# Value columns accumulated beside the modulation, filters and gates beside query and gate columns, in a hybrid mixer block

## The chip, the cores and the metric

The kernel runs on one core of a Trainium2 chip. The core has a matrix engine (PE), a vector engine (DVE), a scalar engine (ACT), a general engine (POOL) and a queue engine (SP), each with its own instruction stream; they meet through semaphores. Loads go from the chip's memory into on-chip memory (SBUF) through DMA queues; PE writes its products into a small accumulator memory (PSUM) of eight banks. The metric is the device time of one execution in microseconds.

## The reference

One layer of a diffusion backbone, float32, with 256 tokens of context and 256 latent tokens of 2048 channels. Cut to what matters here:

```python
mod_l = split(silu(c) @ w_mod + b_mod, 6)         # w_mod [2048, 12288]
mod_c = split(silu(c_ctx) @ w_mod + b_mod, 6)
h_ctx, h_lat = ctx * (1 + mod_c[1]) + mod_c[0], x * (1 + mod_l[1]) + mod_l[0]
hy, q, k, v, o, gates, u, mg = split(h @ w_in)    # w_in [2048, 12304], k, v, u for both streams
y_ml = mlstm(q, k, v, gates, o)                   # q, k through a short convolution
y_s5 = s5(u)                                      # a complex diagonal state space, both directions
y_hy = hyena(hy)                                  # long convolutions with filters from a small network
merged = sum(sigmoid(g) * (y @ w) for g, y, w in branches)    # g: three thirds of mg
x = norm(ALPHA * x + mod_l[2] * (merged @ w_out))
x = norm(ALPHA * x + mod_l[5] * (relu(modulate(x, mod_l[3], mod_l[4]) @ w_ff1) ** 2 @ w_ff2))
```

The first two parts of the modulation are wanted before any product with w_in; the other four are wanted behind the mixer and in the feed-forward part.

## The kernel before

All weights are float32 and pass once through the core in chunks of 512 KB. A chunk is loaded on SP's queue into a tile `wr` (four buffers, L155), split into a high part `wh` by ACT and a low part `wl` by DVE (three buffers each, both at L145 and L149 in `split`), and multiplied by PE in three products for each pair of k and column tile: high by high, high by low, low by high. `lin_w` computes a block of columns of the projection into one PSUM tile `mm`, of which there are two with two banks each; `px` and `aux`, two banks each, serve everything else. A block for both streams is 256 columns wide and has four chunks of four k, a block for the latent stream alone is 512 columns wide and has eight chunks of two k. When a block's products are done a consume function reads the tile. `lin_w_steps` yields between chunks, and `run_steps(steps, n)` runs n chunks of it. Side work is written as generators in three slots; `chunk_done`, behind each chunk, advances each by its rate, so that `with_side(gen, 1.75, 1)` runs 1.75 parts of a generator per chunk. A scheduler then sets a fixed order for each engine from the order in the program and the buffers; an instruction waits for those ahead of it on its engine.

The stages, in the order of the program. `phase0(g)` for g from 0 to 3: `mod_block` streams 16 chunks of the first part of the modulation (four products with the stream's chunk in columns of the array, not split), then `h_group` makes four channel tiles of the modulated and transposed inputs. Beside group g of the modulation stand three key chunks, with the four k that group g - 1 has made; `part` adds the products of four k at a time in SBUF (copy by ACT the first time, then an add by DVE, L1504), since a PSUM tile would be needed for each block otherwise. Then come the last four k of the three key blocks and `k_consume`; the value columns V in 12 chunks with three kinds of side work: `gates`, `mod_late` (the rest of the modulation, by DVE alone at L1226, two products to a chunk, summed over k in the single buffer `mac`; 128 chunks in 16 blocks; PE adds up the rows of `mac` into `px` behind each block) and `hy_filters`; the query columns Q, 12 chunks; `mlstm`; the U columns, 12 chunks, whose consume copies on ACT and issues eight small DMAs for each column tile (L611); the O columns, 12; six hyena chunks; `s5_inject`; the other hyena chunks and 32 chunks of the merge gates (mg, 96 in all, `mg_consume` to DRAM) beside the scan on POOL; 48 more beside `s5_output`, whose first product is at L714; the rest of mg beside `hyena`; the three merges; the product with w_out, ahead of which `need_mods(12)` runs `mod_late` on until 96 of its chunks are done; and the feed-forward part, ff1 and ff2, between which `drain(1)` runs what is left of it.

## Time and profile before

| what | value |
|---|---|
| device time, median of 3 runs | 2071.19 us |
| lowest and highest | 2070.89, 2072.36 us |
| span of the profiled execution | 2066.5 us |
| PE busy | 1908.3 us, 92% |
| DVE busy | 1373.0 us, 66% |
| ACT busy | 799.8 us, 39% |
| POOL busy | 526.1 us, 25% |
| read from memory | 414.58 MB, 211 GB/s with what is written |

The span runs from the first to the last instruction of the profiled execution; the device time has what lies around it as well. Products on PE are pipelined, and a row's duration overlaps that of the next. The table by stage has, for each stretch, the busy time of each engine and in brackets the number of instructions, then PE's granted clock as a share of full speed, and the share of the DMA engines' time.

### The profile page before, as it was taken

What the parts mean: (1) busy time and instruction counts of PE and PEld (TensorE: products, weight loads), DVE (VectorE), ACT (ScalarE), POOL (GpSimd) and SP (SyncE); (2) the same over time, 40 slices, a digit from 0 to 9 for tenths busy, and PEclk for the clock granted to TensorE, in tenths of its full rate; (3) what the DMA queues carried; (4) which work ended last, traced back from release to release, by engine and by line L of the source; (5) the groups of instructions that cost most, each with busy time, mean ns of one, the idle gap of its engine ahead of it and who ended that gap; (6) DMA issues with size and microseconds to landing.
All of it is one profiled execution on the core that took longest, in us unless ns stands there. A gap on an engine that the chain in (4) does not pass through costs nothing.

```text
span 2066.5 us, 34948 instructions
## 1 busy us (share of the span) xinstructions
PE 1908.3 (92%) x14085; PEld 1733.0 (84%) x14085; DVE 1373.0 (66%) x1840; ACT 799.8 (39%) x1066; POOL 526.1 (25%) x656
## 2 busy tenths in 40 slices
PE   6889999999888999589988999799999999999995
PEld 2657988989888898579878978799989899998985
DVE  5567877547989855495688766966665555555556
ACT  1323333236444333234433443544443334444331
POOL 3435211000435799960243410500000000000001
PEclk7889999999999999789999999999999999999998
DMA  9777676766666676447766776577776666667663
GB/s 303 244 246 255 200 230 221 228 183 193 219 193 192 209 243 221 130 141 224 265 210 199 263 264 208 178 237 236 231 245 188 191 186 184 183 182 229 192 185 101
DMA packets 243378, 435.64 MB, mean 211 GB/s; under 512 B 22431, under 2 KB 69225, under 8 KB 242225
## 3 DMA queue, kind: packets, MB, share of 16 engines
q1 hardware_dynamic: 221744, 382.29, 59.1%
q0 software_dynamic: 11968, 43.26, 6.2%
q10 hardware_dynamic: 9504, 7.87, 1.4%
q8 instruction: 110, 1.80, 0.4%
q14 instruction: 52, 0.42, 0.1%
HBM read 414.58 MB, written 21.92 MB: 211 GB/s over the span
## 4 chain that ended last, share of the span: by engine, by line
PE 40%; DVE 9%; POOL 8%; DMA 6%; issue 2%; ACT 1%; POOLq 0%; ACTq 0%; DVEq 0%
PE mm L166 39%; DVE wl L149 3%; POOL sc L678 2%; POOL t L681 2%; DMA wr<-in_w_mod_dram 2%; POOL sc L680 2%; DMA wr<-in_w_out_dram 2%; POOL sc L679 2%; ACT wh L145 1%; DVE t L149 1%; DMA wr<-in_w_in_dram 1%; DVE mac L1226 1%; PE aux L166 1%; DMA wr<-in_w_hy_out_dram 1%; DVE b L707 0%
## 5 line engine op out<-in xcount | busy, mean ns | idle before, releaser
L166 PE MATMUL mm<-t,wh 128*128 128x256 f32 x5888 | 1112.5, 289 | 13.2 <-DVE t L149 7.0
L166 PEld LDWEIGHTS mm<-t,wh 128*128 128x128 f32 x5888 | 937.8, 195 | 39.5 <-issue 13.9
L149 DVE TENSOR_TENSOR wl<-wr,wh 128x1024 fp32r<-128x1024 f32 (+1 forms) x517 | 666.0, 1293 | 392.6 <-ACT wh L145 392.1
L145 ACT ACTIVATE wh<-wr 128x1024 fp32r<-128x1024 f32 (+1 forms) x517 | 546.3, 1058 | 841.2 <-PE mm L166 584.5
L166 PE MATMUL mm<-t,wl 128*128 128x256 f32 x2944 | 849.9, 289 | 19.0 <-DVE wl L149 18.8
L166 PEld LDWEIGHTS mm<-t,wl 128*128 128x128 f32 x2944 | 572.7, 195 | 31.5 <-DVE wl L149 23.2
L1226 DVE SCALAR_TENSOR_TENSOR mac<-wr,sc,mac 128x512 f32<-128x512 f32 x240 | 189.7, 790 | 143.6 <-DMA wr<-in_w_mod_dram 141.0
L166 PE MATMUL mm<-wh,t 128*128 128x512 f32 (+1 forms) x960 | 247.5, 347 | 0.0
L166 PEld LDWEIGHTS mm<-wh,t 128*128 128x128 f32 x960 | 168.2, 189 | 23.3 <-ACT wh L145 1.1
L166 PE MATMUL mm<-wl,t 128*128 128x512 f32 (+1 forms) x480 | 168.3, 351 | 5.3 <-DVE wl L149 5.2
L166 PE MATMUL mm<-wh,ff 128*128 128x512 f32 (+1 forms) x576 | 155.3, 358 | 0.0
L166 PEld LDWEIGHTS mm<-wh,ff 128*128 128x128 f32 x576 | 101.8, 188 | 17.6
L166 PEld LDWEIGHTS mm<-wl,t 128*128 128x128 f32 x480 | 90.8, 189 | 22.3 <-DVE wl L149 11.0
L166 PE MATMUL mm<-wl,ff 128*128 128x512 f32 (+1 forms) x288 | 103.0, 357 | 0.0
L1448 POOL DMA_DIRECT2D t<-in_ln_g_dram x1 | 0.5, 532 | 355.9 <-PE mm L166 355.9
L166 PE MATMUL mm<-ty,wh 128*128 128x256 f32 x384 | 73.3, 289 | 0.0
L166 PE MATMUL mm<-ty,wl 128*128 128x256 f32 x192 | 56.7, 296 | 8.5 <-DVE wl L149 8.3
L166 PEld LDWEIGHTS mm<-ty,wh 128*128 128x128 f32 x384 | 60.9, 192 | 0.9
L166 PEld LDWEIGHTS mm<-wl,ff 128*128 128x128 f32 x288 | 54.2, 188 | 8.8
L1237 POOL DMA_DIRECT2D mrow<-b x8 | 4.0, 500 | 224.0 <-DVE b L1235 224.0
L371 PE MATMUL px<-wr,b 128*32 128x512 f32 x128 | 40.6, 723 | 13.5 <-DMA wr<-in_w_mod_dram 13.5
L166 PE MATMUL aux<-t,t 128*128 128x384 f32 (+3 forms) x160 | 47.2, 411 | 5.4 <-DMA t<-HX 1.9
(458 smaller groups left out, 1937.2 us busy)
## 6 DMA issues: line engine op xcount, KB each, us to landing
wr<-in_w_ff_dram SPq DMA_DIRECT2D x256, 512.0 KB, 4.0
wr<-in_w_in_dram SPq DMA_DIRECT2D x192, 512.0 KB, 4.5
wr<-in_w_mod_dram SPq DMA_DIRECT2D x160, 512.0 KB, 4.8
wr<-in_w_out_dram SPq DMA_DIRECT2D x32, 512.0 KB, 4.6
wh<-in_w_mod_dram SPq DMA_DIRECT2D x16, 512.0 KB, 6.0
wl<-in_w_mod_dram SPq DMA_DIRECT2D x16, 512.0 KB, 6.9
MG<-mg POOLq DMA_DIRECT2D x24, 256.0 KB, 4.4
wr<-in_w_ml_out_dram SPq DMA_DIRECT2D x12, 512.0 KB, 4.5
```

Source lines behind the costliest of these rows:

```text
L145: return self.nc.scalar.activation(out, in_, f, bias=bias, scale=scale)
L149: self.nc.vector.tensor_sub(lo, x, hi.bitcast(F32))
L166: self.nc.tensor.matmul(out, lhsT, rhs, start=start, stop=stop, skip_group_check=True)
L371: nc.tensor.matmul(ps[o:o + 32], self.st[:, k, :], raw[:, kk, :], start=k < 4, stop=k >= KT - 4, skip_group_check=True, tile_position=(0, o))
L678: v.tensor_mul(t1, self.a8[:, 0], S[:, :, :, :, n - 1])
L679: v.tensor_mul(t2, self.a8[:, 1], S[:, :, ::-1, :, n - 1])
L680: v.tensor_add(t1, t1, S[:, :, :, :, n])
L681: v.tensor_add(S[:, :, :, :, n], t1, t2)
L1226: v.scalar_tensor_tensor(acc, x, c, acc, op0=ALU.mult, op1=ALU.add)
L1237: nc.gpsimd.dma_start(self.mrow[which // 3:which // 3 + 1, o:o + 512], brow)
L1448: nc.gpsimd.dma_start(g2r, I["ln2_g"].to_broadcast([P, D]))
```

## The change

`part` takes a list of accumulators in place of one. Beside the three key blocks there are three value blocks with accumulators of their own in SBUF: the fourth tile of `room`, and four half tiles under the tags "mg" (three) and "mac" (one). In `phase0` six steps stand among the 16 modulation chunks of a group, behind chunks 3, 6, 8, 11, 14 and 16, three key and three value chunks in turn; there were three, behind 3, 7 and 11. Behind `k_consume` the last four k of each value block and `v_consume` follow. The side work that stood beside V now stands beside Q and the first 12 chunks of mg, which are called right behind Q; `mod_late` has rate 0.6 there and `hy_filters` 1.2 as before. The later calls of 32, 48 and 96 mg chunks are as they were.

```diff
-                    if n % 4 == 3 and todo:
+                    if n in (3, 6, 8, 11, 14, 16) and todo:
                         step, k0 = todo.pop(0)
                         step(k0)
-            for step, k0 in todo:
-                step(k0)
...
-        def part(i, c0):
-            acc = self.room[i][:, :4, :]
+        def part(accs, c0):
+            n = 4 // len(accs)
...
                 once(k0, True)
-                if k0 == 0:
-                    self.act(acc, ps)
-                else:
-                    nc.vector.tensor_add(acc, acc, ps)
+                for i, acc in enumerate(accs):
+                    p = ps[:, n * i:n * i + n, :]
+                    if k0 == 0:
+                        self.act(acc, p)
+                    else:
+                        nc.vector.tensor_add(acc, acc, p)
...
-            kparts = [part(i, O_K + 256 * i) for i in range(3)]
-            self.ksteps = [step for _, step in kparts]
+            kparts = [part([self.room[i][:, :4, :]], O_K + 256 * i) for i in range(3)]
+            one = lambda tag, bufs: self.t(self.sm, [P, 512], tag, bufs).rearrange("p (s t) -> p s t", s=2)
+            vaccs = [[self.room[3][:, :4, :]], [one("mg", 3), one("mg", 3)], [one("mg", 3), one("mac", 1)]]
+            vparts = [part(a, O_V + 256 * i) for i, a in enumerate(vaccs)]
+            self.ksteps = [step for _, step in kparts + vparts]
...
                     gates = self.gates()
                     next(gates)
+                    for i, (accs, step) in enumerate(vparts):
+                        step(12)
+                        for j, acc in enumerate(accs):
+                            n = 2 // len(accs)
+                            self.v_consume(2 * i + n * j, n, acc)
                     self.with_side(gates, 0.5)
-                    self.with_side(self.mod_late(), 1.75, 1)
+                    self.with_side(self.mod_late(), 0.6, 1)
                     self.with_side(self.hy_filters(), 1.2, 2)
-                    self.lin_w_all(w_in, O_V, W, KT, both, self.v_consume)
+                    self.qT = self.t6([P, CT, T])
+                    self.lin_w_all(w_in, O_Q, W, KT, lat, self.q_consume)
                     self.drain()
-                    self.qT = self.t6([P, CT, T])
-                    self.sides[1][1] = 0.3
-                    self.lin_w_all(w_in, O_Q, W, KT, lat, self.q_consume)
+                    steps = self.lin_w_steps(w_in, O_MG, 3 * D, KT, lat, self.mg_consume)
+                    self.run_steps(steps, 12)
                     self.drain(2)
...
-                steps = self.lin_w_steps(w_in, O_MG, 3 * D, KT, lat, self.mg_consume)
```

How the order moves, first on PE where the U columns begin. Before, `mm_464` is the last block of Q, `aux` rows are the mLSTM's products, and `mm_531` is the first block of U:

```order
L166 MATMUL mm_464_3437<-t32_24_112,wl_479_3541 128x256
L166 MATMUL mm_464_3437<-t32_24_112,wh_478_3540 128x256 x2
L166 MATMUL mm_464_3437<-t32_24_112,wl_479_3541 128x256
L166 MATMUL aux_481_3577<-t6_406_3093,t6_252_1732 128x256 x2
L166 MATMUL aux_481_3577<-t6_406_3093,t6_253_1733 128x256
L166 MATMUL aux_482_3583<-t6_406_3093,t6_252_1732 128x256 x2
L166 MATMUL mm_531_3884<-t32_23_111,wh_533_3887 128x256 x2
L166 MATMUL mm_531_3884<-t32_23_111,wl_534_3888 128x256
L166 MATMUL mm_531_3884<-t32_24_112,wh_533_3887 128x256 x2
```

After, `mm_502` is the second block of mg, `px` the row sum of a late modulation block, the `aux` rows products of the filters and of the mLSTM; `mm_569` (not shown) is the first block of U:

```order
L166 MATMUL mm_502_3791<-t32_24_112,wh_515_3892 128x256
L166 MATMUL mm_502_3791<-t32_24_112,wl_516_3893 128x256
L166 MATMUL px_578_4349<-mac_464_3603,ones_8_79 1x512
L166 MATMUL aux_473_3626<-ty_347_2815 128x384
L166 MATMUL aux_474_3629<-ty_347_2815 128x384
L166 MATMUL aux_482_3669<-ty_344_2812,b4_343_2810 128x384
L166 MATMUL aux_481_3668<-ty_344_2812,b4_343_2810 128x384
L166 MATMUL aux_490_3711<-ty_344_2812,b4_343_2810 128x384
L166 MATMUL aux_489_3710<-ty_344_2812,b4_343_2810 128x384
```

And later on PE, in the scan, with the last rows of a hyena block `mm_1026`:

```order
L169 MATMUL aux_782_6160<-consts_14_90,s5q_778_6128 128x128 x2
L169 MATMUL aux_782_6160<-consts_14_90,s5q_779_6135 128x128 x2
L166 MATMUL mm_1026_7492<-t32_24_112,wl_1051_7626 128x256
L166 MATMUL mm_1026_7492<-t32_24_112,wh_1050_7625 128x256 x2
L166 MATMUL mm_1026_7492<-t32_24_112,wl_1051_7626 128x256
L166 MATMUL mm_502_3791<-t32_24_112,wh_1061_7683 128x256 x2
L166 MATMUL mm_502_3791<-t32_24_112,wl_1062_7684 128x256
```

The block `mm_502` stops after four of its eight chunks ahead of U, and goes on behind `mm_1026`.

On ACT where the first block of U is read out, before (`mm_531`):

```order
L145 ACTIVATE wh_548_4070<-wr_547_4068 128x1024
L145 ACTIVATE wh_555_4151<-wr_554_4149 128x1024
L145 ACTIVATE wh_562_4219<-wr_561_4217 128x1024
L145 ACTIVATE wh_567_4278<-wr_566_4276 128x1024
L145 ACTIVATE b2_551_4126<-mm_531_3884 128x8x64
L611 DMA UD_1_72<-b2_551_4126 16x8x64 x8
L145 ACTIVATE b2_552_4137<-mm_531_3884 128x8x64
L145 ACTIVATE wh_572_4340<-wr_571_4338 128x1024
L611 DMA UD_1_72<-b2_552_4137 16x8x64 x8
```

and after (`mm_569`):

```order
L145 ACTIVATE wh_587_4420<-wr_586_4418 128x1024
L145 ACTIVATE wh_595_4505<-wr_594_4503 128x1024
L145 ACTIVATE wh_599_4563<-wr_598_4561 128x1024
L145 ACTIVATE wh_604_4625<-wr_603_4623 128x1024
L145 ACTIVATE b2_591_4480<-mm_569_4232 128x8x64
L611 DMA UD_1_72<-b2_591_4480 16x8x64 x8
L145 ACTIVATE b2_592_4491<-mm_569_4232 128x8x64
L611 DMA UD_1_72<-b2_592_4491 16x8x64 x8
L145 ACTIVATE wh_610_4689<-wr_609_4687 128x1024
```

The copies `b2<-mm` stand behind the same number of weight splits in both; there is one split fewer between the second copy and its DMA issues.

On DVE where ff1 ends and ff2 begins, before (`wl_2106` is ff2's first split, `px_2100` the row sum of the last block of the modulation):

```order
L1226 SCALAR_TENSOR_TENSOR mac_2049_15120<-wr_2095_15533,sc_17_97,mac_2049_15120 128x512
L149 TENSOR_TENSOR wl_2091_15476<-wr_2089_15473,wh_2090_15475 128x1024
L1226 SCALAR_TENSOR_TENSOR mac_2049_15120<-wr_2095_15533,sc_17_97,mac_2049_15120 128x512
L1226 SCALAR_TENSOR_TENSOR mac_2049_15120<-wr_2097_15542,sc_17_97,mac_2049_15120 128x512
L149 TENSOR_TENSOR wl_2094_15506<-wr_2092_15503,wh_2093_15505 128x1024
L1226 SCALAR_TENSOR_TENSOR mac_2049_15120<-wr_2097_15542,sc_17_97,mac_2049_15120 128x512
L1226 SCALAR_TENSOR_TENSOR mac_2049_15120<-wr_2098_15546,sc_17_97,mac_2049_15120 128x512 x2
L1226 SCALAR_TENSOR_TENSOR mac_2049_15120<-wr_2099_15550,sc_17_97,mac_2049_15120 128x512 x2
L149 TENSOR_TENSOR wl_2106_15566<-wr_2104_15563,wh_2105_15565 128x1024
L149 TENSOR_TENSOR wl_2109_15584<-wr_2107_15581,wh_2108_15583 128x1024
L1235 TENSOR_TENSOR b2_2101_15556<-b2_2101_15556,px_2100_15554 1x512
```

and after, from behind the bias add of block 14 (it reads `px_2102`) and the first product of block 15, `mac_2104` (L1224); `wl_2119` is ff2's first split:

```order
L1400 TENSOR_TENSOR b4_2099_15535<-b4_2099_15535 128x1024
L1226 SCALAR_TENSOR_TENSOR mac_2104_15554<-wr_2105_15555,sc_17_97,mac_2104_15554 128x512
L1226 SCALAR_TENSOR_TENSOR mac_2104_15554<-wr_2106_15559,sc_17_97,mac_2104_15554 128x512
L149 TENSOR_TENSOR ff_1982_14508<-b4_2099_15535,ff_1982_14508 128x1024
L1226 SCALAR_TENSOR_TENSOR mac_2104_15554<-wr_2106_15559,sc_17_97,mac_2104_15554 128x512
L1226 SCALAR_TENSOR_TENSOR mac_2104_15554<-wr_2107_15563,sc_17_97,mac_2104_15554 128x512 x2
L1226 SCALAR_TENSOR_TENSOR mac_2104_15554<-wr_2108_15567,sc_17_97,mac_2104_15554 128x512 x2
L1226 SCALAR_TENSOR_TENSOR mac_2104_15554<-wr_2109_15571,sc_17_97,mac_2104_15554 128x512 x2
L1226 SCALAR_TENSOR_TENSOR mac_2104_15554<-wr_2110_15575,sc_17_97,mac_2104_15554 128x512 x2
L1226 SCALAR_TENSOR_TENSOR mac_2104_15554<-wr_2111_15579,sc_17_97,mac_2104_15554 128x512 x2
L1226 SCALAR_TENSOR_TENSOR mac_2104_15554<-wr_2112_15583,sc_17_97,mac_2104_15554 128x512
L149 TENSOR_TENSOR wl_2119_15599<-wr_2117_15596,wh_2118_15598 128x1024
```

All but one of block 15's products now stand ahead of ff2's first split, behind the row sum of block 14; on PE that row sum stands as the last product ahead of ff2's first.

On SP where the merges end and w_out begins, before:

```order
L155 DMA wr_1672_12400<-in_w_hy_out_dram 128x2x512
L155 DMA wr_1678_12443<-in_w_hy_out_dram 128x2x512
L155 DMA wr_1681_12473<-in_w_hy_out_dram 128x2x512
L155 DMA wr_1684_12503<-in_w_mod_dram 128x2x512
L155 DMA wr_1685_12507<-in_w_hy_out_dram 128x2x512
L155 DMA wr_1695_12560<-in_w_out_dram 128x2x512
L155 DMA wr_1698_12578<-in_w_out_dram 128x2x512
L155 DMA wr_1701_12596<-in_w_out_dram 128x2x512
```

and after:

```order
L155 DMA wr_1679_12447<-in_w_hy_out_dram 128x2x512
L155 DMA wr_1682_12477<-in_w_hy_out_dram 128x2x512
L155 DMA wr_1685_12518<-in_w_mod_dram 128x2x512
L155 DMA wr_1686_12522<-in_w_mod_dram 128x2x512
L155 DMA wr_1687_12526<-in_w_mod_dram 128x2x512
L155 DMA wr_1688_12530<-in_w_mod_dram 128x2x512
L155 DMA wr_1689_12534<-in_w_mod_dram 128x2x512
L155 DMA wr_1690_12538<-in_w_mod_dram 128x2x512
L155 DMA wr_1691_12542<-in_w_mod_dram 128x2x512
L155 DMA wr_1700_12564<-in_w_out_dram 128x2x512
L155 DMA wr_1703_12582<-in_w_out_dram 128x2x512
```

Seven modulation chunks now stand in a row ahead of the first chunk of w_out.

## Rows read from the trace of the kernel before

**Rows 1.** The page's head and busy times: engine, us, share of the span, instructions.

```profile
span 2066.5 us, 34948 instructions
...
PE 1908.3 (92%) x14085; PEld 1733.0 (84%) x14085; DVE 1373.0 (66%) x1840; ACT 799.8 (39%) x1066; POOL 526.1 (25%) x656
```

**Rows 2.** Stages up to U: length; PE, PEld, DVE, ACT, POOL busy; clock, DMA, GB/s.

```profile
48.40:86.00 37.60, 36.24 (x288) 27.86 (x286) 17.46 (x28) 14.14 (x29) 10.33 (x12) 0.89 0.86 255
86.00:97.50 11.50, 5.29 (x36) 3.71 (x33) 11.50 (x14) 4.65 (x15) 10.82 (x9) 0.71 0.65 223
97.50:131.60 34.10, 32.46 (x251) 23.86 (x251) 15.76 (x24) 7.13 (x15) 4.15 (x4) 0.95 0.86 279
131.60:143.20 11.60, 5.89 (x45) 3.26 (x45) 11.60 (x13) 3.84 (x15) 8.03 (x9) 0.51 0.57 194
143.20:176.00 32.80, 32.46 (x264) 22.65 (x265) 28.97 (x34) 8.35 (x28) 20.86 (x21) 0.91 0.67 221
...
196.00:300.00 104.00, 101.50 (x775) 92.64 (x774) 82.37 (x191) 32.34 (x44) 22.03 (x38) 1.00 0.66 205
300.00:349.00 49.00, 48.73 (x347) 43.22 (x346) 35.17 (x54) 22.35 (x32) 5.99 (x12) 1.00 0.72 230
349.00:421.00 72.00, 72.00 (x562) 67.50 (x561) 42.20 (x57) 17.11 (x23) 2.45 (x5) 1.00 0.75 223
```

**Rows 3.** ACT's timeline in U: start, us, what, idle before and its releaser.

```profile
371.24 1.06 ACT L145 ACTIVATE wh<-wr 128x1024 fp32r<-128x1024 f32 x1 [5.94 <-PE mm L166]
377.00 1.06 ACT L145 ACTIVATE wh<-wr 128x1024 fp32r<-128x1024 f32 x1 [4.70 <-PE mm L166]
382.76 1.06 ACT L145 ACTIVATE wh<-wr 128x1024 fp32r<-128x1024 f32 x1 [4.70 <-PE mm L166]
383.72 0.58 ACT L145 ACTIVATE b<-mm 128x512 f32<-128x512 f32 x1
384.33 3.88 ACTq L611 DMA_DIRECT2D UD<-b  x8
388.26 0.60 ACT L145 ACTIVATE b<-mm 128x512 f32<-128x512 f32 x1 [3.96 <-issue]
```

**Rows 4.** DVE's groups by line: count, busy us and mean ns, idle before.

```profile
L149 DVE TENSOR_TENSOR wl<-wr,wh 128x1024 fp32r<-128x1024 f32 x516 | 665.3, 1294 | 392.6 <-ACT wh L145 392.1
L1226 DVE SCALAR_TENSOR_TENSOR mac<-wr,sc,mac 128x512 f32<-128x512 f32 x240 | 189.7, 790 | 143.6 <-DMA wr<-in_w_mod_dram 141.0
L1400 DVE TENSOR_TENSOR b<-b 128x1024 f32<-128x1024 f32 x16 | 19.5, 1218 | 0.0
...
L1504 DVE TENSOR_TENSOR ty<-ty,mm 128x1024 f32<-128x1024 f32 x9 | 11.0, 1217 | 10.6 <-PE mm L166 10.6
```

**Rows 5.** ACT's timeline in ff1.

```profile
1490.22 1.06 ACT L145 ACTIVATE wh<-wr 128x1024 fp32r<-128x1024 f32 x1 [1.77 <-PE mm L166]
1493.10 1.06 ACT L145 ACTIVATE wh<-wr 128x1024 fp32r<-128x1024 f32 x1 [1.82 <-PE mm L166]
```

**Rows 6.** A stretch behind the norm, by stage.

```profile
1300.00:1325.00 25.00, 20.82 (x145) 19.20 (x145) 22.05 (x41) 14.66 (x28) 15.78 (x12) 0.81 0.53 179
```

**Rows 7.** PE's timeline where the S5 output begins.

```profile
871.12 2.19 PE L714 MATMUL aux<-s5q,b 128*64 128x128 f32 x18 [21.62 <-ACT b L145]
```

**Rows 8.** The scan's stretch and hyena's, by stage.

```profile
702.00:849.50 147.50, 135.94 (x1092) 133.91 (x1090) 85.67 (x78) 52.47 (x56) 139.12 (x212) 0.98 0.72 227
...
987.00:1110.00 123.00, 107.57 (x745) 98.16 (x744) 99.33 (x118) 43.70 (x61) 52.41 (x51) 0.93 0.67 225
```

**Rows 9.** SP's timeline between ff1 and ff2.

```profile
1487.51 7.87 SPq L155 DMA_DIRECT2D wr<-in_w_mod_dram  x4
```

**Rows 10.** PE's timeline where ff2 begins.

```profile
1503.68 0.51 PE L166 MATMUL mm<-wl,t 128*128 128x512 f32 x1 [0.48 <-DVE wl L149]
```

**Rows 11.** DVE's timeline there.

```profile
1505.38 0.67 DVE L1235 TENSOR_TENSOR b<-b,px 1x512 f32<-1x512 f32 x1
```

**Rows 12.** The page's DMA issues: KB each, median us from issue to landing.

```profile
wr<-in_w_mod_dram SPq DMA_DIRECT2D x160, 512.0 KB, 4.8
```

More of the change, by code (lines that the diff above doesn't have):

```diff
@@ L1500, in step @@
                 once(k0, True)
-                if k0 == 0:
-                    self.act(acc, ps)
-                else:
-                    nc.vector.tensor_add(acc, acc, ps)
-            return acc, step
+                for i, acc in enumerate(accs):
[4 more added lines that the diff above has]
+                        nc.vector.tensor_add(acc, acc, p)
+            return accs, step
         with self.scope("yp") as self.yp:
             self.room = [self.ty() for _ in range(4)]
-            kparts = [part(i, O_K + 256 * i) for i in range(3)]
-            self.ksteps = [step for _, step in kparts]
+            kparts = [part([self.room[i][:, :4, :]], O_K + 256 * i) for i in range(3)]
[3 more added lines that the diff above has]
+            self.ksteps = [step for _, step in kparts + vparts]
             with self.scope("p0a") as self.br:
@@ L1543, in run @@
                         step(12)
-                        self.k_consume(2 * i, 2, acc)
+                        self.k_consume(2 * i, 2, acc[0])
                     vt = self.t(pv, [P, 3265], "vt", 1)
```

## The prediction

> **What bounds the kernel now.** I read the page's busy table first: in a span of 2066.5 us TensorE (PE) is busy 1908.3, VectorE (DVE) 1373.0 [rows 1]. PE is nearly the bound of the whole, so a moved product costs what it cost before unless it lands in PE's idle time, and a new gap in PE is paid in full. Then the table by stage [rows 2], which says where that idle time is. In the modulation's stage (48.4 to 176 us) the reader should look at PE's busy time beside each stretch's length: 36.24 of 37.60, 32.46 of 34.10, 32.46 of 32.80 while modulation chunks stream, and 5.29 of 11.50 and 5.89 of 11.60 at the two boundaries between groups, where DVE is busy throughout. In all 15.3 us are idle. In the value stage PE is busy 101.5 of 104, in the query stage 48.7 of 49, in the U stage 72.0 of 72: all PE-bound. The sum is made against the span plus what lies around it, 2071.2 - 2066.5 = 4.7 us, which I leave alone; that total is the median of the runs shown.
>
> **The move of nine value chunks into the modulation's stage.** A chunk of both streams has 48 products and comes each 5.76 us (the first three ACT rows of the U stage [rows 3], 371.24, 377.00, 382.76). Twelve value chunks were 69 us; nine, 9 x 5.76 = 52 us, now stand beside the modulation, and three stay behind as the last k. What they can gain is the 15.3 us idle. They cannot have the clock back for nothing either: the granted clock was 0.89, 0.71, 0.95, 0.51 and 0.91 in the five stretches [rows 2]; weighting PE's busy time with one minus these gives 4.0 + 1.5 + 1.6 + 2.9 + 2.9 = 13 us. So the gain lies between 0 and 15.3 + 13 = 28. I take 6: the sixth step of each group stands after the last modulation chunk and ahead of the group's transposes, so one chunk of 5.76 us can lie in a boundary, but the boundary is DVE's, and DVE gets more there: a chunk's split, 1.29 us, and an add from PSUM, 1.22 us [rows 4]. The two boundaries could take up 2 x 5.76; half of it is 6. **-6.** The adds (six more in this stage, with three copies on ACT) are 6 x 1.22 = 7 us of DVE, hidden by its idle time, since it is busy 17.5 of 37.6 and 15.8 of 34.1 there; without that cover they would be PE's to wait for.
>
> The Trainium skill (Perfetto Trace Analysis, Optimization Strategy) says that where the most-contended engine changes over time, interleaving the regimes can help. Here the trace does not bear it out in full: the stage that should lend time is PE-bound in its streaming stretches itself. By the rule the term would be the whole 28; it is rival one.
>
> **Gates and filters moved from the value columns to query and gate columns.** The 12 gate chunks behind Q were 24-product chunks at 2.87 us (ACT's splits for such chunks in the feed-forward part stand at 1490.22 and 1493.10 [rows 5]). PE's work there is moved, not changed. DVE's is packed closer: counted instruction by instruction in the order and priced at their kinds' means, DVE has 64 us beside 59 us of PE in the twelve gate chunks, and 47 beside 49 in Q. 64 - 59 = **+5**; 0 if DVE works ahead, 12 if Q's share is late too. In the value stage it was 82.4 of 104 [rows 2], so cover is thin but there.
>
> **The accumulator that is held.** This is the term I trust most. The gate columns go in blocks of eight chunks, and the steps now called behind Q are twelve. So the second block stops half done (mm_502), and its PSUM tile, one of the two of "mm", stays occupied through the U, O and hyena columns until the scan, where the order resumes it. U, O and hyena blocks then have one tile: PE cannot begin a block before the last has been read out. In the U stage the trace of before shows what stands in that readout on ACT [rows 3]: the split of the next chunk's weights, 1.06 us (it is ahead in the order, and waits for the buffer of the last chunk), a copy of 0.58, eight DMA issues of 3.88, and the second copy, 0.60, ending 6.1 us after the split began; with 0.3 to start PE, 6.4 us. Before, none of it was on the path: PE went on in the other tile, 72.0 of 72.0 busy. U has three blocks; behind the third come the mLSTM's fp32 products, which cover it. So 2 x 6.4 = 12.8, and some 3 for the clock, which falls after gaps of this size (0.81 in a stretch with 4.2 us idle in 25 [rows 6]). **+16**, bounds 0 (readout put ahead of everything) and 20. The O, hyena and glu boundaries have ACT copies alone, and side products between blocks: **+3** (0 to 10).
>
> The Trainium skill (Perfetto Trace Analysis, Matmuls) says that independent groups should rotate through different PSUM banks, so that the readout of one overlaps the next group's products. The trace of before shows only the rotating case; no row shows a single tile, and by the rule the price is the 16 above, without it 0.
>
> **Scan and S5 output.** Between the last injection product and the first L714 product there were 47 chunks, now 49: gate chunks that stay are still called as 32 and 48. PE waits 21.62 us before L714 [rows 7], for a chain through POOL, which is busy 139.1 of 147.5 in the scan [rows 8]. Two chunks more, 2 x 2.87, fill the wait: **-6** (0 to -10).
>
> **The tail of the gates.** Beside hyena 4 chunks stay where 16 were. Those 34.5 us went ahead to Q; hyena's stretch (107.6 busy of 123 [rows 8]) keeps its own idle 15.4 us and loses cover. Against it, PE work of the same amount now ends earlier, and its region ends by PE's products: **-5** (0 to -10) for the shorter stretch, **+3** (0 to 6) for the merges that then catch up with hyena's last DVE work.
>
> **The late modulation.** Its rate is 0.6 beside Q and the gates in place of 1.75 beside V. Before w_out, 96 of its 128 chunks must be done. Before, 103 were; now 89, and seven stand in a row on SP's queue ahead of w_out's first. Four in a row take 7.87 us on the queue [rows 9], so seven take 14; buffers hold three product chunks, 8.6 us, of cover, partly used by the accumulation behind it: 14 - 6 = **+8** (3 to 14).
>
> Between ff1 and ff2 the rest is drained: four chunks before, eleven now. Four were just covered: PE waited 0.48 us for the first split of ff2 [rows 10]. Of eleven, the last eight are block 15, whose one buffer `mac` is read by the row sum of block 14; in the order that product (px_2102) stands behind all of ff1 on PE. So DVE begins block 15 as ff1 ends, and does the bias add (0.67 [rows 11]), L1400's product and ff's, 1.22 each, and fifteen of its sixteen products ahead of ff2's first split: 0.7 + 1.2 + 1.2 + 15 x 0.79 [rows 4] = 15.0, and 0.4 to PE: 15.4 of idle PE, with 2 for the clock **+17** (9 if block 15's loads are the only cost, 20).
>
> **Sum.** -6 + 5 + 16 + 3 - 6 - 5 + 3 + 8 + 17 = **+35**: 2071.2 + 35 = 2106.
>
> **Rivals.** *One: the regimes interleave.* Its place is the modulation's stage: value chunks fill the boundaries and keep the clock, -28 in place of -6. With -6, -5, +5, +3 and +3 as above that is -28, and it decides the sign once U, w_out's loads and ff2, 41 in the sum, cost less than that; at their low ends (0, 3 and 9) the time is 2071 - 28 + 12 = 2055. For it: 28 us of idle time and slow clock that can be seen. Against it: DVE, not PE, fills the boundaries, and the tile that is held and the row sum that is late stand in the order itself. 8%. The Trainium skill's section on interleaving regimes, cited above, speaks for it.
>
> *Two: gains and losses meet.* The same 28, with U at its 16 and the others at their low ends, 3 and 9: 2071 - 28 + 28 = 2071. For and against as in the first. 6%.
>
> *Three: slower still.* The gate chunks behind Q become DVE-bound over both stretches (+12), U's readout is late by a further DMA issue, and the modulation's own buffers, shared with value chunks on the same SP queue, arrive later: a modulation chunk takes 4.8 us to land [rows 12], and four buffers serve both. It decides once DVE's backlog passes one chunk, 2.87 us. With the high ends of the terms: 2071 + 12 + 20 + 10 + 6 + 14 + 20 - 12 = 2141. 10%.
>
> *The change not doing what it says* is excluded for the move itself: the order has value and key chunks in turn with the modulation's in all groups but the first.
>
> **How the numbers follow.** Forecast 76%, its own range 2080 to 2130 from the ends of U, ff2 and phase terms taken not all at once. The range 2076 to 2130 leaves out rivals one and two (14%) and most of the third. Faster by over 0.2% (4 us, about what a measurement of this kernel can tell from no change): 8%; within: 6%; slower: 86%.
>
> **What would show it.** Right: the modulation's stage some 46 us longer and K-to-Q shorter by 52; two gaps of about 6 us on PE in U, released by ACT's b<-mm; a gap of about 15 us before ff2's first product, released by DVE's split, with fifteen L1226 rows ahead of it; a run of seven modulation loads ahead of w_out. Wrong: a stage lengthened by under 30 us, U's blocks following without a gap, or PE waiting less than 5 us at ff2. What would make the forecast wrong as a whole is PE's idle time in the modulation's stage being filled to the last.

## The result and the profile after

The changed kernel takes 2160.39 us (median of four runs, 2158.24 to 2166.15) against 2071.04 for the kernel before: a ratio of 1.0432, 95% interval 1.0412 to 1.0453, or 89 us more. The forecast was 2106 with a range up to 2130. The sign was right; the loss is two and a half times as large as the sum said. The profiled execution has a span of 2164.4 us and took 2166.15.

The page's busy times after, to set beside [rows 1]:

```profile
span 2164.4 us, 34967 instructions
...
PE 1940.0 (90%) x14085; PEld 1757.4 (81%) x14085; DVE 1387.4 (64%) x1855; ACT 809.1 (37%) x1074; POOL 522.0 (24%) x656
```

PE has as many instructions and 32 us more busy time (the same products at a lower clock, mostly); the other 66 us are new idle time. The table by stage, columns as in [rows 2]: the modulation's stage (the first two rows), the last four k of K and V, Q, the twelve gate chunks, and U:

```profile
48.40:88.00 39.60, 38.53 (x293) 29.73 (x292) 17.49 (x26) 14.51 (x22) 0.63 (x2) 0.99 0.83 236
88.00:212.00 124.00, 113.67 (x964) 89.63 (x963) 87.62 (x99) 36.08 (x99) 60.83 (x56) 0.94 0.65 212
212.00:265.00 53.00, 51.32 (x413) 48.36 (x412) 29.77 (x60) 20.34 (x36) 18.30 (x35) 0.97 0.55 174
265.00:311.00 46.00, 46.00 (x382) 44.91 (x381) 36.61 (x80) 20.97 (x25) 4.17 (x7) 1.00 0.80 252
311.00:388.00 77.00, 58.67 (x364) 46.32 (x363) 52.86 (x116) 31.61 (x44) 6.36 (x12) 0.91 0.50 163
388.00:498.00 110.00, 86.96 (x570) 76.12 (x569) 49.80 (x69) 17.28 (x21) 7.86 (x15) 0.86 0.60 185
```

The modulation's stage looks as hoped, with a clock of 0.99 and 0.94. The two last rows don't: PE is idle for 18 and 23 us in them, where before it was idle for 0.3 in Q and not at all in U [rows 2].

For what follows, the stages are measured alike in all kernels: from ACT's split of a stage's first weight chunk to that of the next stage's, and where gate chunks (mg) were called elsewhere, 2.87 us for each is taken out. In us, with the profiled execution's own span at the foot:

| stage | before | after | held_only | gf_moved | gf_held | late_moved | sides8 | mg8 |
|---|---|---|---|---|---|---|---|---|
| modulation | 133.1 | 168.7 | 133.8 | 134.5 | 134.2 | 132.8 | 132.8 | 168.1 |
| K to Q, with the mg chunks there | 173.0 | 141.8 | 172.2 | 172.0 | 177.6 | 174.1 | 168.2 | 135.7 |
| U | 71.8 | 110.3 | 89.2 | 90.3 | 116.4 | 74.8 | 96.5 | 86.9 |
| O | 63.8 | 67.5 | 68.4 | 61.8 | 68.1 | 61.1 | 59.6 | 59.0 |
| hyena columns, 80 mg, scan, S5 | 490.9 | 509.6 | 503.4 | 495.1 | 505.2 | 494.2 | 501.8 | 499.3 |
| glu to last merge | 174.3 | 192.4 | 172.0 | 169.4 | 176.9 | 188.2 | 186.3 | 185.0 |
| w_out | 96.4 | 93.0 | 97.8 | 96.4 | 97.2 | 94.0 | 95.9 | 93.5 |
| ff1 | 209.2 | 230.5 | 208.2 | 208.8 | 209.2 | 225.7 | 227.2 | 225.1 |
| span | 2066.5 | 2164.4 | 2099.7 | 2075.8 | 2132.7 | 2102.9 | 2119.0 | 2102.9 |

A stage that begins with the rest of the stage ahead of it (U, behind the filters) carries that rest.

The gaps that the forecast named are there. PE and then ACT and DVE where U's first block is read out (to set beside [rows 3]):

```profile
448.50 0.77 PE L166 MATMUL mm<-t,wh 128*128 128x256 f32 x2 [8.74 <-DVE ty L613]
...
483.75 0.77 PE L166 MATMUL mm<-t,wh 128*128 128x256 f32 x2 [6.62 <-DVE ty L613]
...
438.74 1.06 ACT L145 ACTIVATE wh<-wr 128x1024 fp32r<-128x1024 f32 x1 [4.70 <-PE mm L166]
439.70 0.58 ACT L145 ACTIVATE b<-mm 128x512 f32<-128x512 f32 x1
440.31 3.93 ACTq L611 DMA_DIRECT2D UD<-b  x8
444.29 0.60 ACT L145 ACTIVATE b<-mm 128x512 f32<-128x512 f32 x1 [4.01 <-DVE mac L1226]
...
447.27 0.75 DVE L1226 SCALAR_TENSOR_TENSOR mac<-wr,sc,mac 128x512 f32<-128x512 f32 x1 [3.40 <-DMA wr<-in_w_mod_dram]
447.94 0.42 DVE L613 COPY ty<-mm 128x256 f32<-128x256 f32 x1
```

ACT's readout ends 6.15 us after its split began, as costed from [rows 3]. But the tile has a second reader, DVE's copy L613, which in the order stands behind a late modulation product, and that waits 3.40 us for its load: the gap is 8.74, and DVE's copy ends it, not ACT's as the forecast had it.

Ahead of w_out, SP's seven loads in a row, and PE; between ff1 and ff2, DVE's chain and PE:

```profile
1253.60 16.07 SPq L155 DMA_DIRECT2D wr<-in_w_mod_dram  x7
...
1280.19 0.80 PE L166 MATMUL mm<-wh,t 128*128 128x512 f32 x1 [12.01 <-ACT wh L145]
...
1587.46 0.68 DVE L1235 TENSOR_TENSOR b<-b,px 1x512 f32<-1x512 f32 x1 [3.63 <-PE px L166]
1592.17 7.05 DVE L1226 SCALAR_TENSOR_TENSOR mac<-wr,sc,mac 128x512 f32<-128x512 f32 x9
1601.36 0.75 DVE L1226 SCALAR_TENSOR_TENSOR mac<-wr,sc,mac 128x512 f32<-128x512 f32 x1 [0.36 <-DMA wr<-in_w_mod_dram]
1603.72 1.23 DVE L149 TENSOR_TENSOR wl<-wr,wh 128x1024 fp32r<-128x1024 f32 x1 [1.61 <-ACT wh L145]
...
1603.74 0.80 PE L166 MATMUL mm<-wh,t 128*128 128x512 f32 x1 [16.32 <-ACT wh L145]
...
1572.39 24.07 SPq L155 DMA_DIRECT2D wr<-in_w_mod_dram  x11
1602.63 1.06 ACT L145 ACTIVATE wh<-wr 128x1024 fp32r<-128x1024 f32 x1 [11.88 <-DMA wr<-in_w_ff_dram]
```

At ff2 the wait that ends last is not DVE's. DVE is done with block 15's products of this stretch at 1602.11 us, but ACT's split of ff2's first chunk waits 11.88 us for a load that stands behind the eleven modulation loads on SP's queue and ends at 1603.69, just ahead of PE's product. Those loads in turn wait 16.4 us in all for DVE's products, which free the buffers.

What the forecast did not name stands between Q and the first gate block, on PE and ACT:

```profile
321.73 0.60 PE L166 MATMUL aux<-consts,gz 128*8 128x128 f32 x2 [3.42 <-DVE gz L866]
333.02 2.92 PE L166 MATMUL aux<-ty,ty 128*128 128x384 f32 x4 [6.71 <-DVE ty L1064]
...
326.35 0.59 ACT L145 ACTIVATE DT<-aux 8x512 f32<-8x512 f32 x1 [8.29 <-PE aux L166]
331.62 0.42 ACT L145 ACTIVATE ty<-ty 128x256 f32<-128x256 f32 x1 [4.68 <-DVE ty L312]
331.94 1.00 ACT L145 ACTIVATE t<-mm,mlcb,mlcw 128x256 f32<-128x256 f32 x2
```

ACT waits 8.29 us for the gates' product and 4.68 for the filters' sine; the readout of Q's block (`t<-mm`), which must end before a gate block gets the tile, stands behind both.

### The profile page after: what moved, and what is told of

The parts are those of the page before. It is cut to its first block, busy times and chain, and to the rows that moved or that the text cites. A ratio compares the mean times of both kernels' runs of the same rounds, so it can differ in the third digit from the quotient of the medians.

```text
span 2164.4 us, 34967 instructions
## 1 busy us (share of the span) xinstructions
PE 1940.0 (90%) x14085; PEld 1757.4 (81%) x14085; DVE 1387.4 (64%) x1855; ACT 809.1 (37%) x1074; POOL 522.0 (24%) x656
## 5 line engine op out<-in xcount | busy, mean ns | idle before, releaser
L149 DVE TENSOR_TENSOR wl<-wr,wh 128x1024 fp32r<-128x1024 f32 x517 | 662.5, 1285 | 422.7 <-ACT wh L145 421.7
L145 ACT ACTIVATE wh<-wr 128x1024 fp32r<-128x1024 f32 x517 | 546.5, 1058 | 908.3 <-PE mm L166 729.3
L1226 DVE SCALAR_TENSOR_TENSOR mac<-wr,sc,mac 128x512 f32<-128x512 f32 x240 | 195.1, 813 | 151.7 <-DMA wr<-in_w_mod_dram 149.0
L166 PEld LDWEIGHTS mm<-wl,t 128*128 128x128 f32 x480 | 92.1, 192 | 16.4 <-DVE wl L149 3.6
L166 PE MATMUL mm<-ty,wh 128*128 128x256 f32 x384 | 78.8, 302 | 6.1 <-DVE t L1277 3.3
L166 PE MATMUL mm<-ty,wl 128*128 128x256 f32 x192 | 58.8, 307 | 6.0 <-DVE wl L149 6.0
```

Of the source, the lines that this page charges most:

```text
L145: return self.nc.scalar.activation(out, in_, f, bias=bias, scale=scale)
L149: self.nc.vector.tensor_sub(lo, x, hi.bitcast(F32))
L166: self.nc.tensor.matmul(out, lhsT, rhs, start=start, stop=stop, skip_group_check=True)
L1226: v.scalar_tensor_tensor(acc, x, c, acc, op0=ALU.mult, op1=ALU.add)
```

## The experiments

**The half-done block alone.** `held_only` is the kernel before, with four gate chunks behind Q:

```diff
+                    steps = self.lin_w_steps(w_in, O_MG, 3 * D, KT, lat, self.mg_consume)
+                    self.run_steps(steps, 4)
                     self.drain(2)
...
-                steps = self.lin_w_steps(w_in, O_MG, 3 * D, KT, lat, self.mg_consume)
```

> The kernel before, with four mg chunks (half a block) called right behind Q; nothing else of the change. Held-tile theory: the half-done block keeps one of the two mm tiles through U, O and the hyena columns, so PE shows two gaps of 6 to 9 us inside U, about 1 us at the O and hyena blocks, and the time is 2071 + 16 to 25 = 2087 to 2096 us. Rival (the gaps in U of the changed kernel come from its DVE order, not from the tile): no gap over 2 us in U and a time of 2066 to 2076 us.

Measured: 2104.07 us, ratio 1.0152 (1.0114 to 1.0191), 31 us. PE's waits in U, and one in the injection:

```profile
402.69 0.77 PE L166 MATMUL mm<-t,wh 128*128 128x256 f32 x2 [6.94 <-DVE ty L613]
436.57 0.76 PE L166 MATMUL mm<-t,wh 128*128 128x256 f32 x2 [8.02 <-DVE ty L613]
...
585.35 0.45 PE L169 MATMUL aux<-consts,s5q 128*128 128x128 f32 x1 [9.37 <-DVE s5q L647]
```

The held tile by itself makes U's two gaps (the U stage is 17.4 us longer, forecast 16), so the rival falls. The stage of O takes 4.6 more and that of hyena and scan 12.5, so that the 31 us are above the 16 to 25 expected. A product of the injection comes to wait 9.37 us there, for DVE; that the single tile is behind this wait is not shown.

**Whole blocks.** `mg8`, the changed kernel with one whole block behind Q:

```diff
-                    self.run_steps(steps, 12)
+                    self.run_steps(steps, 8)
```

> The changed kernel with 8 mg chunks behind Q in place of 12, so that the block is finished and no tile is held; the other four chunks run beside hyena. Held-tile theory: the gaps in U (8.7, 6.6 and 2.3 us in the changed kernel) go, and if the longer hyena stretch (19 us over before) is the same cause, up to that much more: 2160 - 17 to 36 = 2124 to 2143 us. Rival (the gaps come from where DVE's readout stands in its order): 2155 to 2165 us, with the gaps in U still there.

Measured: 2106.91 us, ratio to before 1.0164 (1.0136 to 1.0192). From 2160 that is 53 us, more than either theory gave. Stages of 40 us from 380 on:

```profile
380.00:420.00 40.00, 40.00 (x259) 32.77 (x259) 25.80 (x39) 8.13 (x12) 5.88 (x11) 1.00 0.66 216
420.00:460.00 40.00, 40.00 (x328) 39.00 (x327) 19.44 (x26) 7.92 (x9) 1.49 (x3) 1.00 0.74 208
460.00:500.00 40.00, 40.00 (x245) 31.05 (x245) 19.33 (x27) 15.69 (x27) 0.48 (x1) 1.00 0.59 170
```

PE has no idle time there, at a clock of 1.00; in the changed kernel it idled 23 us in U at 0.86. So four chunks in another place are worth more than half of the whole loss.

**The late modulation's rate.** `late_rate`, the changed kernel with

```diff
-                    self.with_side(self.mod_late(), 0.6, 1)
+                    self.with_side(self.mod_late(), 1.2, 1)
```

> The changed kernel with mod_late at 1.2 parts a chunk in place of 0.6 beside Q and the twelve mg chunks, so that about as many of its chunks are done ahead of w_out and of ff2 as before the change. Theory of the forced runs: the 12.0 us gap ahead of w_out and the 16.3 us gap ahead of ff2, with 5 us of slower clock, go; DVE gets 14 chunks x 1.58 = 22 us more beside Q and mg, of which a half or less is on the path: 2160 - 33 + 0 to 11 = 2127 to 2138 us. Rival (DVE is the bound beside Q and mg, and what is saved behind is paid there): 2150 to 2165 us.

Measured: 2139.58 us, ratio 1.0325 (1.0295 to 1.0356): 21 us back, between the theories. The forced runs are gone (ff1's stage 211.0, glu to the last merge 174.8), 37 us; and the front is 17 us longer (Q 61.2 for 46.4): about half of what is saved is paid there.

**The gates earlier.** `gates_early`, the changed kernel with the gates' generator started ahead of the last three value chunks:

```diff
                     next(gates)
+                    self.with_side(gates, 1.0)
                     for i, (accs, step) in enumerate(vparts):
...
-                    self.with_side(gates, 0.5)
```

> The changed kernel with the generator of the gates started ahead of the last three value chunks, one part a chunk, in place of behind them at half a part. Theory: the 16 us that PE loses between Q and the first mg block (gaps of 3.4, 6.7 and 2.2 us and smaller) come from the gates' chain PE to ACT to DVE, which stands on ACT ahead of the readout of Q's block, and so of the mm tile: 2160 - 10 to 18 = 2142 to 2150 us. Rival (the filters' sine chain alone holds ACT there): under 5 us, 2155 to 2163 us, with the same gaps.

Measured: 2163.95 us, ratio 1.0441 (1.0412 to 1.0471): no gain. The stretch of the twelve gate chunks fell from 76.8 to 58.8 us, as the theory had it, but U's grew from 110.3 to 124.0 and Q's from 46.4 to 50.2. The chain on ACT makes part of that gap, but from U's first split to its first product, where the filters' rest stands, it is 35.3 us in place of 25.7, and U's blocks take 4 us more. As a theory of the time it falls.

**Side work moved, value columns left.** `sides8` is the kernel before with the side work beside Q and eight gate chunks:

```diff
+                    self.lin_w_all(w_in, O_V, W, KT, both, self.v_consume)
                     self.with_side(gates, 0.5)
-                    self.with_side(self.mod_late(), 1.75, 1)
+                    self.with_side(self.mod_late(), 0.6, 1)
                     self.with_side(self.hy_filters(), 1.2, 2)
-                    self.lin_w_all(w_in, O_V, W, KT, both, self.v_consume)
...
+                    self.run_steps(steps, 8)
```

> The kernel before with the side work alone moved: twelve value chunks stand where they stood, bare; gates, mod_late (0.6) and filters run beside Q and eight mg chunks, a whole block. Against mg8 it differs by the value chunks alone. Theory: the nine value chunks beside the modulation gain the 16 us read from the two traces (that stage 35.6 us longer for 51.8 us of chunks), so this kernel takes 2107 + 16 = 2123 us, and moving the side work costs some 50 us against before. Rival (the gain is given back later, the sides' move costs 35): 2100 to 2112 us.

Measured: 2116.7 us (2106.6 to 2120.76), ratio 1.0212 (1.0172 to 1.0252). Against mg8 the value chunks thus gain 10 us by the medians and 16 by the two spans. The two intervals overlap, so that the size is open between 0 and 16; the modulation's stage itself is 16 us better in both traces (35.3 and 35.6 us more for 51.8 of chunks).

**The rate where DVE seems idle.** `mg8_orate` is mg8 with the rate 1.6 from O until the scan; `mg16_orate` has sixteen gate chunks behind Q besides; `mg16_orate_f` has the filters at 0.8:

```diff
-                    self.sides[1][1] = 0.6
+                    self.sides[1][1] = 1.6
                     self.oT = self.ty()
...
-                    self.run_steps(steps, 8)
+                    self.run_steps(steps, 16)
...
-                    self.with_side(self.hy_filters(), 1.2, 2)
+                    self.with_side(self.hy_filters(), 0.8, 2)
```

> mg8 with the rate of mod_late at 1.6 in place of 0.6 from the O columns until the scan, where DVE is idle half the time, so that 106 of its chunks are done by w_out. Theory: the forced runs ahead of w_out and ff2 go (12 + 16 us and 5 of slower clock, and with them the merges' 10 us), at a cost of 0 to 10 beside O and the first hyena chunks: 2107 - 43 + 0 to 10 = 2064 to 2080 us. Rival (DVE is what the injection chain waits for, and 17 chunks more push it back by their 27 us): 2085 to 2100 us.

> mg8_orate with sixteen mg chunks behind Q, two whole blocks, and none beside hyena. Theory: eight chunks more (23 us of PE) cover the rest of the filters that PE otherwise runs bare ahead of U, 10 to 15 us; hyena loses that cover and its own waits show, 0 to 15: between 15 us faster and as fast as mg8_orate. Rival (hyena's chain of DVE and POOL becomes the bound of its stretch): 10 to 20 us slower than mg8_orate.

> mg16_orate with the filters at 0.8 parts a chunk in place of 1.2, so that their 21 parts spread over 26 chunks in place of 18. If the rate, parts per 2.87 us chunk where it was per 5.76 us, is what makes PE wait beside Q and mg: 5 to 15 us faster than mg16_orate. Rival (the chain of the filters is as long at any rate): within 4 us of it.

Measured: 2101.07, 2108.08 and 2112.8 us, ratios 1.0146 (1.0109 to 1.0182), 1.0177 (1.0144 to 1.021) and 1.019 (1.0154 to 1.0226). In mg8_orate the forced runs are gone (16 us less from glu to the last merge, 22 in ff1), but O takes 74.6 in place of 59.0 and the next stage 510.0 in place of 499.3, so that 6 us are left: the rival, nearly. The intervals of the three overlap; neither sixteen chunks nor slower filters gain anything that shows. But sixteen chunks, four more than the change calls there, take 2108 us where its twelve take 2160. The rate of mod_late differs too, but is worth 6 us by mg8_orate; so the 53 us between mg8 and the changed kernel come from the half-done block, and not from the number of gate chunks ahead of U.

**One kind of side work each.** On the kernel before, `late_moved` moves mod_late alone, `gf_moved` gates and filters alone:

```diff
-                    self.with_side(self.mod_late(), 1.75, 1)
...
-                    self.sides[1][1] = 0.3
+                    self.with_side(self.mod_late(), 0.95, 1)
                     self.lin_w_all(w_in, O_Q, W, KT, lat, self.q_consume)
```

```diff
+                    self.with_side(self.mod_late(), 1.75, 1)
+                    self.lin_w_all(w_in, O_V, W, KT, both, self.v_consume)
                     self.with_side(gates, 0.5)
-                    self.with_side(self.mod_late(), 1.75, 1)
                     self.with_side(self.hy_filters(), 1.2, 2)
-                    self.lin_w_all(w_in, O_V, W, KT, both, self.v_consume)
...
+                    self.run_steps(steps, 8)
```

> The kernel before with mod_late alone moved from beside V to beside Q, at a rate that leaves 89 of its chunks done by w_out and eleven to drain ahead of ff2, as in the changed kernel; gates, filters and value columns stay. Theory of the forced runs: the gaps of 12 us ahead of w_out and 16 ahead of ff2, with 5 of slower clock, and some 10 us in the merges, are the lateness alone: 2071 + 25 to 43 = 2096 to 2114 us. Rival (DVE, relieved beside V, gives it back): 2071 to 2088 us.

> The kernel before with gates and filters alone moved to beside Q and eight mg chunks (a whole block); mod_late and the value columns stay. Theory: beside 24-product chunks of 2.87 us DVE and ACT have half the room for them that they have beside 48-product chunks of 5.76 us, and the stages until the scan's end take 20 to 30 us more, as they do with all side work moved (26): 2091 to 2101 us. Rival (those 26 us are mod_late's, whose DVE work now stands where the injection waits for DVE): 2066 to 2077 us.

Measured: late_moved 2104.8 us, ratio 1.0152 (1.0111 to 1.0193), 31 us; gf_moved 2082.77 us, ratio 1.0037 (1.0017 to 1.0056), 8 us. PE in late_moved ahead of w_out and of ff2:

```profile
1215.58 0.79 PE L166 MATMUL mm<-wh,t 128*128 128x512 f32 x1 [10.50 <-ACT wh L145]
...
1535.22 0.79 PE L166 MATMUL mm<-wh,t 128*128 128x512 f32 x1 [16.27 <-ACT wh L145]
```

The lateness alone makes both gaps, 27 us of the 31; nothing comes back beside V and Q (the K to Q stage is 174.1 for 173.0). Gates and filters cost less than expected: 18.5 us in U's stage, which begins with the filters' rest, and 4 behind it, against 5 saved in the merges and 7 at the very end. These 7 are not theirs: the last write lands 12.7 us behind PE's last product here and 12.8 before, but a DRAIN of POOL's sequencer that closes the program takes 2.32 us here and 10.81 before. `v1` below, which leaves gates and filters beside V, has the short one too. What sets its length is open; without it gates and filters cost some 15 us.

**Do the parts add?** `held_late` is late_moved with held_only's four chunks, `gf_held` is gf_moved with twelve chunks in place of eight.

> late_moved with the four mg chunks (half a block) behind Q as in held_only: both losses in one kernel, nothing else of the change. Apart they took 31.5 and 31.5 us. If they add: 2071 + 63 = 2134 us. If they raise each other, as the changed kernel against mg8 suggests (53 us for the held tile there, 31.5 in held_only): 2145 to 2160 us.

> gf_moved with twelve mg chunks behind Q in place of eight, so that a half-done block holds a tile; value columns and mod_late as before the change. Apart the two cost 31.5 us (held_only) and 8 us (gf_moved). If they add: 2071 + 40 = 2111 us. If the rest of the filters and the held tile meet ahead of U and in it, which the 53 us between mg8 and the changed kernel suggest: 2125 to 2140 us.

Measured: held_late 2139.07 us, ratio 1.0324 (1.0283 to 1.0366), 67 us: lateness and held tile add in the total. By stage they do not: the hyena and scan stage takes 492.6 us in held_late for 494.2 in late_moved, so that the 12.5 of held_only there do not come with the tile in every kernel. gf_held 2135.5 us, ratio 1.0303 (1.0274 to 1.0332), 63 us where the sum is 39: gates and filters and a held tile cost 24 us more together than apart, give or take 11 by the three intervals. One of U's gaps in it, with ACT's and DVE's rows in that gap:

```profile
481.09 8.68 ACTq L611 DMA_DIRECT2D UD<-b  x8
491.10 1.54 DVE L1226 SCALAR_TENSOR_TENSOR mac<-wr,sc,mac 128x512 f32<-128x512 f32 x2 [4.66 <-DMA wr<-in_w_mod_dram]
493.12 0.77 PE L166 MATMUL mm<-t,wh 128*128 128x256 f32 x2 [13.52 <-DVE ty L613]
```

In this gap the eight DMA issues between ACT's two copies take 8.68 us, with two pauses of 2.4 us among them, where they took 3.88 [rows 3], and DVE's copy stands behind late modulation products that wait 4.66 us for their load. Why the issues pause is open.

By the table, the 24 lie in the K to Q stage (5.6 more than gf_moved), U (26 more, where the held tile alone made 17) and the merges (7.5 more). What links them in each stage was not taken apart.

**A smaller move.** `v1` is the kernel before with one value block of three beside the modulation and the side work left beside the other eight V chunks; `v1b` puts its steps at other places:

```diff
-                    if n % 4 == 3 and todo:
+                    if n in (3, 7, 11, 15) and todo:
...
+            vacc, vstep = part(3, O_V)
+            self.ksteps = [step for _, step in kparts] + [vstep]
...
+                    self.with_side(self.mod_late(), 1.75, 1)
                     for i, (acc, step) in enumerate(kparts):
...
+                    vstep(12)
+                    self.v_consume(0, 2, vacc)
-                    self.with_side(gates, 0.5)
-                    self.with_side(self.mod_late(), 1.75, 1)
-                    self.with_side(self.hy_filters(), 1.2, 2)
+                    self.with_side(gates, 0.75)
+                    self.with_side(self.hy_filters(), 1.5, 2)
```

```diff
-                    if n in (3, 7, 11, 15) and todo:
+                    if n in (3, 8, 13, 16) and todo:
```

> The kernel before with one of the three value blocks accumulated beside the modulation (three value chunks in place of nine; the fourth tile of room as accumulator), the other eight V chunks with gates and filters at 0.75 and 1.5 parts, mod_late at 1.75 from the last key chunks on. Theory: a third to a half of the gain of nine, 4 to 6 us, and the side work keeps its 48-product chunks: 2063 to 2068 us. Rival (eight chunks don't cover the side work, which shows behind Q): 2075 to 2085 us.

> v1 with the four steps of a group behind modulation chunks 3, 8, 13 and 16 in place of 3, 7, 11 and 15, so that the last stands at the boundary between groups as in the changed kernel. If filling that boundary is where value chunks gain: 3 to 6 us under v1, 2063 to 2068 us. Rival (DVE, not PE, fills the boundary, and one chunk more there only moves it): within 2 us of v1's ratio of 0.998, 2065 to 2069 us against 2071, or 1 to 4 us slower.

Measured: v1 2071.16 us, ratio 0.9982 (0.9962 to 1.0003), no difference; v1b 2065.79 us, ratio 0.9963 (0.9945 to 0.998), faster than both kernels of this case by a little. The stretches where the boundaries of [rows 2] were, first in v1b, then in v1, and POOL's last instruction before and in v1b:

```profile
86.00:98.00 12.00, 11.77 (x95) 9.89 (x94) 2.45 (x2) 4.24 (x5) 0.66 (x1) 1.00 0.96 345
...
132.00:144.00 12.00, 11.92 (x124) 10.25 (x122) 10.56 (x10) 4.64 (x13) 8.75 (x9) 1.00 0.80 253
...
86.00:98.00 12.00, 12.00 (x128) 9.32 (x120) 7.98 (x9) 5.20 (x11) 1.92 (x3) 1.00 0.83 278
132.00:144.00 12.00, 11.44 (x102) 9.47 (x101) 9.33 (x7) 2.66 (x9) 6.42 (x7) 1.00 0.79 253
...
2054.67 1.45 POOL L1433 TENSOR_TENSOR x<-x,t 128x384 f32<-128x384 f32 x1
2056.65 1.45 POOL L1433 TENSOR_TENSOR x<-x,t 128x384 f32<-128x384 f32 x1
```

PE is busy through these 12 us each, at full clock, where it was busy half of the time; but so it is in v1, which gained nothing, and in both the stretch from 144 to 176 us has 5 us of idle PE. By the one trace of each, the boundary step is not what makes v1b faster. Its modulation stage takes 11.2 us more for 17.3 us of chunks, a gain of 6, and U's stage gives 8 back; PE's last product ends at 2047.6 us, later than before (2045.5). What makes the span shorter, 2061.8 for 2066.5, is the DRAIN behind POOL's last instruction, 2.32 us for 10.81. v1's trace has the short DRAIN as well (2.23 us); with the long one v1 would be the slower kernel.

## Why the prediction was wrong, step by step

Measured costs stand as ratio times 2071 us.

- **Value chunks beside the modulation, forecast -6.** -10 by the medians of mg8 and sides8. The stage grew by 35.6 us, not 46, within the bounds; PE's idle time fell only from 15.3 to 11.4 us; weighted as in the prediction, the slow clock's share fell from 13 to 7 (0.99 and 0.94 for 0.51 to 0.95). Sign and size about right, but the 6 were idle time in two boundaries, and more than half of what came is the clock: the size is in part luck.
- **Gates and filters, forecast +5.** +8 alone (gf_moved), or some 15 without the shorter end of the program, which no term had. But the step was wrong in kind: it set DVE's summed time beside PE's, 64 against 59, where DVE is busy 52.86 us in that stretch and PE 58.67, of 77. The wait is a chain PE, ACT, DVE and back, and what it held up was ACT's readout of Q.
- **The held accumulator, forecast +16 and +3.** The mechanism was right in U and shown alone by held_only: 17.4 there. DVE's copy ended the waits, not ACT's, and no run shows the 0.3 us to start PE (0.14 us lie between the copy's end and the product). The term was mis-sized behind U: 17 in O and the scan's stage where 3 stood, 31 in all, though how much of these 17 the tile makes is not shown. And it was added as if the other terms did not touch it: with gates and filters moved it costs 55 (gf_held less gf_moved), with mod_late moved 36. This is the step that failed, by 36 us of the 54 by which the sum was short. What held one of U's gaps in gf_held is shown above; what links the two costs is open.
- **Scan and S5 output, forecast -6.** The wait ahead of L714 was 20.43 us for 21.62 [rows 7], so -1: two chunks more did not fill it.
- **The gates' tail, forecast -5 and +3.** The stage from glu to the last merge is 18 us longer after, of which 14 are in late_moved; the other 4 stand where -2 did.
- **The late modulation, forecast +8 and +17.** 12.01 and 16.32 us of gap; 31 us alone with the clock and the merges. The sum was 6 too small. The seven loads took 16.07 us on the queue, not the 14 scaled from [rows 9]. At ff2 the size was met by a chain that was only half right: DVE's products of block 15 run there as forecast, but they hold PE back through the buffers of ff2's loads, and ACT's split releases it, not DVE's.

The measured parts add up to -10 + 8 + 31 + 24 + 31 = 84, of 89. The rest is within the intervals of the parts.

The third rival, slower still at 2141, had the direction and not the cause: DVE was not the bound of the gate chunks (52.86 of 77 us busy), and a modulation chunk landed no later (4.5 us by the page, for 4.8).

## What to carry to other kernels

A loop that stops in the middle of an accumulation keeps its PSUM tile until it goes on: count in whole blocks, since four chunks too many made 53 of the 89 us here. Side work whose rate is given per chunk doubles its density when it moves from 5.76 us chunks to 2.87 us chunks; look then for a readout that stands behind it on an in-order engine, and not only at the engine with the largest sum. (A lower rate of the filters alone gained nothing here.) When each term of a sum is a wait around the same few buffers, price the pairs too: here one pair was worth 24 us. And look at where a variant's gain lies in its trace: v1b's is at the end of the program, behind all that was changed.

## What the runs showed of the hardware

Short gaps cost clock as well. In the changed kernel's U stage, from behind the filters' rest to behind the gap of 8.74 us:

```profile
405.00:410.00 5.00, 2.36 (x10) 0.97 (x8) 2.95 (x5) 0.00 (x0) 0.54 (x1) 1.00 0.80 278
413.00:420.00 7.00, 7.00 (x39) 6.46 (x38) 1.50 (x2) 0.00 (x0) 0.52 (x2) 0.64 0.44 166
420.00:430.00 10.00, 10.00 (x85) 10.00 (x85) 4.14 (x5) 2.12 (x2) 0.00 (x0) 1.00 0.57 159
440.00:448.50 8.50, 0.00 (x0) 0.03 (x1) 5.06 (x9) 0.88 (x2) 0.00 (x0) 0.62 0.79 225
448.50:452.00 3.50, 3.50 (x16) 3.50 (x17) 1.10 (x2) 0.00 (x0) 0.49 (x1) 0.50 0.63 163
452.00:456.00 4.00, 4.00 (x35) 4.00 (x34) 1.50 (x2) 0.00 (x0) 0.48 (x1) 0.97 0.30 52
```

A clock of 1.00 is the level of 2.4 GHz and 0.50 that of 1.2. PE is busy for 2.36 of 5 us up to 410, and from 413 to 420 the clock is 0.64; from 420 to 430, with PE busy, it is at 1.00. In the gap it falls again (0.62 on the mean), and PE's first 3.5 us behind it run at 0.50: besides the 8.74 us some 2 us (an estimate from these rows). Before, with PE busy throughout U, the clock was 1.00 [rows 2].

The end of the program has two lengths. In all 16 kernels with a trace the last write lands 12.7 to 12.8 us behind PE's last product, but POOL's closing DRAIN takes 10.8 to 11.0 us in four of them (before, held_only, late_moved, held_late) and 2.2 to 2.3 in the others. What decides it is open.
